# Six modulation chunks of layer 0 moved ahead of the latent attention

## Chip, cores and metric

The kernel runs on one core of a Trainium2 chip. The metric is the device time of one execution in microseconds (us). The time before is 2217.39 us, the median of three runs from 2213.5 to 2222.52 us. The profile shown here is of one further execution, which took 2211.2 us; its trace covers a span of 2209.4 us.

The engines are named as in the profile: PE is TensorE's matmul, PEld its weight load, DVE is VectorE, ACT is ScalarE, POOL is GpSimd and SP is SyncE, which issues most of the DMAs. "Load" below is a DMA from HBM.

## The reference

Two transformer blocks work one after the other on 256 tokens of 1024 features, each with two layers. The change lies in the first layer (layer 0) of the first block, in what feeds its modulation. A conditioning vector `c` (and one for the context tokens, `c_ctx`) is turned into six vectors of 1024 numbers: shift, scale and gate for the mixer, and shift, scale and gate for the feed-forward part.

```python
mod = silu(c) @ w_mod[l] + b_mod[l]          # 1024 -> 6 x 1024
sh1, sc1, g1, sh2, sc2, g2 = split(mod, 6)
u = modulate(rms_norm(h, g_pre_mix), sh1, sc1)
y = even_mixer(u, ...)                        # delta rule + latent attention, then w_out
h = h + g1 * rms_norm(y, g_post_mix)
u = modulate(rms_norm(h, g_pre_ffn), sh2, sc2)
h = h + g2 * rms_norm(swiglu(u, ...), g_post_ffn)
```

The mixer of layer 0 is made of two parts that share one input projection: a gated delta rule in both directions over chunks of 64 tokens, a recurrence with eight heads, and a multi-head latent attention (MLA). Their outputs are concatenated and multiplied by `w_out`.

## The kernel before

Context and latent tokens are handled together as four tiles of 128 tokens. A product of a float32 input and a weight is done as three matmuls on parts cut in two (`mm3`, L554 to L556): a weight tile is loaded by SP, cast to its high part by ACT (L270), and VectorE or GpSimd subtracts to get the low part (L272).

The modulation of layer 0 is done in chunks of 512 columns, numbered 0 to 11; `n // 2` is the vector that a chunk belongs to, in the order shift, scale, gate of the mixer, then of the feed-forward. `mod_chunk` (L361) computes one. It loads `w_mod` in four loads of 512 KB (L370), each into a weight buffer of the tag `wraw`. Each load is used by two float32 matmuls (L373; the trace shows four records for them) whose stationary side is 32 columns wide, with the first two columns the two conditioning vectors; the eight matmuls of a chunk go round the four groups of 32 rows of one PSUM bank, `gv`. ACT copies the bank out (L375). For a gate (chunks 4, 5, 10, 11) a small matmul adds the four groups up (L379), POOL loads the bias (L381), VectorE adds it (L382) and multiplies by a gain (L400), and POOL stores the row to DRAM (L401). For a shift or scale (the others) four small matmuls (L386) give columns, and VectorE adds the bias (L389) and writes the coefficients (L413 or L415).

Chunks 0 to 3 (shift and scale of the mixer) are done at the start, since the first norm needs them. Chunks 4 to 9 (gate of the mixer, shift and scale of the feed-forward) are done in `l0_mixer`, in the loop that the change moves. Chunks 10 and 11 follow later, on VectorE.

In the program, `l0_mixer` goes: input norm, small input projection, delta-rule preparation (`gdn_conv`, `gdn_gate`, `gdn_matrices`), inversion of the triangular matrices (`gdn_invert`), the recurrence of eight steps for each tile and direction (`gdn_run`) and its end (`gdn_post`); then `l0_mla`, then the chunks. `layer0` goes on with `gdn_out` and the output projection (`linear_tok` on `w_out_even`, L1896).

The order on an engine is not that of the program. The kernel is built with

```python
with tile.TileContext(nc, schedule_with_timeline_sim=True) as tc:
```

so a scheduler lays the instructions of each engine in a fixed order when the kernel is built; the order in which the program issues the work enters into it, but does not alone decide it. Each engine then carries out its list in that order. Two resources matter here. From L1850 on, the weight buffers are only the two of the pool `w`, so a load waits until the one before the last has been used. The PSUM pool has one `gv` bank; `mod_chunk` and the attention both use it (in `attend`, L700 puts the reciprocal sums there), and they take it in the order of the program.

In the second half of `gdn_matrices` SP loads two tiles `gE` for each token tile (L1050), VectorE multiplies (L1056) and SP stores the products as `Qd` (L1058). The recurrence loads them again, one 256 KB load `gQ` for each step (L1172).

Of the kernel before, what the change touches and what calls it, by code (L numbers as in the profile page):

```python
# [128 lines left out]
def sbt(K, shape, dt=F32, tag=None, bufs=1, pool=None):  # L129
    return (pool or K.sb).tile(shape, dt, name=nm(K, tag or "u"), tag=tag or nm(K, "one"), bufs=bufs)  # L130
# [69 lines left out]
def bank(K, kind):  # L200
    kind = K.alias.get(kind, kind)
    return K.ps[kind].tile([128, 512], F32, name=nm(K, kind), tag=kind, bufs=K.kinds[kind])
# [158 lines left out]
def mod_chunk(K, W, pool, l, n, pm=None):  # L361

    nc = K.nc
    pm = pm or pool
    ps = bank(K, "gv")
    for g in range(0, 8, KG):
        raw = W.raw()
        nc.sync.dma_start(raw, K.ins["w_mod"][l][g * 128:(g + KG) * 128, n * 512:(n + 1) * 512].rearrange("(k p) n -> p k n", p=128))  # L370
        for k in range(KG):
            j = (g + k) % 4
            nc.tensor.matmul(ps[32 * j:32 * j + 32, :], K.cl[:, g + k, :], raw[:, k, :], start=(g + k < 4), stop=(g + k >= 4))  # L373
    row = sbt(K, [128, 512], F32, "mrow", 1, pm)
    nc.scalar.copy(row, ps)  # L375
    sel = K.c("sel")
    ps = bank(K, "gv")
    if n // 2 in (2, 5):
        nc.tensor.matmul(ps[:2, :], sel, row, start=True, stop=True)  # L379
        b = sbt(K, [128, 512], F32, "mrow", 1, pm)[:2]  # L380
        nc.gpsimd.dma_start(b, K.ins["b_mod"][l, n * 512:(n + 1) * 512].partition_broadcast(2))  # L381
        nc.vector.tensor_tensor(b, ps[:2, :], b, op=ALU.add)  # L382
        mod_gate(K, pool, l, n, b, 2)
        return
    for f in range(4):
        nc.tensor.matmul(ps[:, 2 * f:2 * f + 2], row[:, f * 128:(f + 1) * 128], sel, start=True, stop=True)  # L386
    v = sbt(K, [128, 4, 2], F32, "mcols", 2, pm)
    b = K.col("b_mod")[:, l * 48 + 4 * n:l * 48 + 4 * n + 4]
    nc.vector.tensor_tensor(v, ps[:, :8].rearrange("p (f s) -> p f s", s=2), bc(b, [128, 4, 2], 2), op=ALU.add)  # L389
    mod_cols(K, l, n, v.rearrange("p f s -> p (f s)"), 2)  # L390


def mod_gate(K, pool, l, n, ps, ns):

    nc = K.nc
    i, half = n // 6, n % 2
    cs = slice(half * 512, half * 512 + 512)
    g = sbt(K, [2, 512], F32, "mgr", 1, pool)[:ns]
    nc.gpsimd.dma_start(g, K.ins["g_post"][l, i, cs].partition_broadcast(ns))
    nc.vector.tensor_tensor(g, ps[:ns, :], g, op=ALU.mult)  # L400
    nc.gpsimd.dma_start(K.grow[l][i][:ns, cs], g)  # L401


def mod_cols(K, l, n, ps, ns):

    nc = K.nc
    sec, half = divmod(n, 2)
    f0 = sec * 8 + half * 4
    dst = K.modc[l][:, :ns, f0:f0 + 4]
    src = ps[:, :4 * ns].rearrange("p (f s) -> p s f", s=ns)  # L410
    if sec in (1, 4):
        gain = K.col("pre")[:, (l * 2 + sec // 3) * 8 + half * 4:(l * 2 + sec // 3) * 8 + half * 4 + 4]
        nc.vector.scalar_tensor_tensor(dst, src, 1.0, bc(gain, [128, ns, 4], 1), op0=ALU.add, op1=ALU.mult)  # L413
    else:
        nc.vector.tensor_copy(dst, src)  # L415
# [318 lines left out]
def bc(ap, shape, axis):  # L734
    return ap.unsqueeze(axis).to_broadcast(shape)
# [481 lines left out]
def gdn_run(K):  # L1217
    K.owritten = set()
    for i in range(4):
        for d in range(2):  # L1220
            t = i if d == 0 else (1, 0, 3, 2)[i]
            ops = gdn_operands(K, d, t)
            for a in ((0, 1) if d == 0 else (1, 0)):
                gdn_state(K, d, i == 0 and a == d, t, a, *ops, K.S[d])
# [562 lines left out]
def l0_mixer(K, W, Om):  # L1787
    nc = K.nc
    with Pool(K, "c0") as c0:
# [8 lines left out]
        with Pool(K, "qkv"):  # L1798
            K.small = cut(K, [128, 4, 448])
            K.qkv = [cut(K, [128, 4, 512]) for _ in range(3)]  # L1800
            with Pool(K, "pq") as pP:
# [55 lines left out]
                with Pool(K, "g3"):  # L1857
                    gdn_run(K)
                    gdn_post(K)
                    with Pool(K, "mla", "right"):  # L1860
                        l0_mla(K, Om)
                        for n in range(4, 10):
                            mod_chunk(K, W, K.po, 0, n)


def layer0(K):
# [5 lines left out]
    with Banks(K, {"g": 3, "s": 2, "tp": 1, "po": 1, "gv": 1}, {"acc": "s", "aux": "g"}):  # L1872
        l0_mixer(K, W, Om)
# [297 lines left out]
```

## Time and profile before

| | |
|---|---|
| time of the runs (median of 3) | 2217.39 us |
| the profiled execution | 2211.2 us |
| its span in the trace | 2209.4 us |
| PE busy | 2035.4 us, 92% of the span |
| VectorE busy | 1319.9 us, 60% |
| ScalarE busy | 921.9 us, 42% |
| mean granted clock of PE | 0.936 of full speed |

The page shows the span in 40 slices of 55 us, with one digit each for an engine's busy share in tenths and for the clock granted to PE. A busy PE is not always PE at its peak: matmuls are pipelined, and at a granted clock of 0.5 it counts as busy with half the work done. In timelines, each line gives the start, the duration, the engine, the source line, what is written and read, and how many instructions were put together; in brackets is the engine's idle time before it and what ended it. Source lines are those of the kernel before.

### The profile page before, as it was taken

How to read it: one execution, taken by the hardware profiler on the slowest of the kernel's cores; microseconds unless marked ns; L12 is line 12 of the kernel's file. 1: busy time of each engine (PE TensorE's matmuls, PEld its weight loads, DVE VectorE, ACT ScalarE, POOL GpSimd, SP SyncE). 2: the span in 40 equal slices, each digit the busy share in tenths (PEclk: the TensorE clock that was granted, in tenths of full speed). 3: DMA queues.
4: the chain of work that ended last, by engine and by line, in shares of the span. 5: the costliest groups of instructions: out<-in, count | busy, mean ns of one | idle time of the engine just before them, and what ended most of it. 6: DMA issues, size and time to landing. Idle time of an engine off the chain costs nothing.

```text
span 2209.4 us, 31163 instructions
## 1 busy us (share of the span) xinstructions
PE 2035.4 (92%) x11656; PEld 1640.6 (74%) x11656; DVE 1319.9 (60%) x2737; ACT 921.9 (42%) x1612; POOL 241.2 (11%) x312
## 2 busy tenths in 40 slices
PE   6989898857999999979987999999899999989998
PEld 3777677614887877867656888898688879868886
DVE  5665566702678674463856556585675467566644
ACT  4533433402522223443435544455454345545532
POOL 2211112100100000020311000210200021020000
PEclk9999599957999999989969999999899999989999
DMA  8343300155267663222304557350566535145561
GB/s 273 91 111 82 116 11 16 59 170 171 85 204 234 223 200 105 96 88 67 96 20 152 154 151 241 111 145 20 162 198 188 158 117 162 44 153 167 185 190 68
DMA packets 186952, 291.90 MB, mean 132 GB/s; under 512 B 28472, under 2 KB 75704, under 8 KB 186800
## 3 DMA queue, kind: packets, MB, share of 16 engines
q1 hardware_dynamic: 172720, 272.54, 39.6%
q0 software_dynamic: 5472, 16.13, 2.2%
q10 hardware_dynamic: 8608, 1.23, 0.4%
q8 instruction: 92, 1.51, 0.3%
q14 instruction: 60, 0.49, 0.1%
HBM read 281.44 MB, written 8.41 MB: 131 GB/s over the span
## 4 chain that ended last, share of the span: by engine, by line
PE 81%; DVE 6%; DMA 5%; issue 3%; ACT 3%; POOL 1%; SPq 0%; ACTq 0%; DVEq 0%; POOLq 0%
PE acc L554 18%; PE acc L556 18%; PE acc L555 18%; PE s L554 2%; PE s L555 2%; PE s L556 2%; PE gv L373 2%; DMA wraw<-in_w_mod_dram 2%; PE po L1531 1%; PE tp L1531 1%; PE po L690 1%; PE tp L891 1%; PE aux L729 1%; PE aux L489 1%; PE g L1200 1%
## 5 line engine op out<-in xcount | busy, mean ns | idle before, releaser
L272 DVE TENSOR_TENSOR wlo<-wraw,whi 128x512 fp32r<-128x512 f32 (+4 forms) x772 | 483.1, 669 | 301.2 <-ACT whi L270 284.4
L270 ACT CAST whi<-wraw 128x1024 fp32r<-128x1024 f32 (+4 forms) x420 | 413.6, 990 | 491.2 <-PE acc L556 204.2
L554 PE MATMUL acc<-whi,u 128*128 128x512 f32 (+3 forms) x1320 | 511.5, 390 | 21.5 <-ACT whi L270 13.2
L555 PE MATMUL acc<-wlo,u 128*128 128x512 f32 (+3 forms) x1320 | 509.4, 388 | 0.8 <-DVE wlo L272 0.7
L556 PE MATMUL acc<-whi,u 128*128 128x512 f32 (+3 forms) x1320 | 507.9, 386 | 1.5 <-DVE u L307 1.5
L554 PEld LDWEIGHTS acc<-whi,u 128*128 128x128 f32 x1320 | 253.2, 192 | 72.7 <-ACT whi L270 15.1
L556 PEld LDWEIGHTS acc<-whi,u 128*128 128x128 f32 x1320 | 252.6, 191 | 51.7 <-DVE u L307 3.8
L555 PEld LDWEIGHTS acc<-wlo,u 128*128 128x128 f32 x1320 | 252.7, 192 | 51.2 <-DVE wlo L272 3.6
L554 PE MATMUL acc<-u,whi 128*128 128x512 f32 (+1 forms) x480 | 169.5, 360 | 1.8 <-ACT u L306 1.7
L556 PE MATMUL acc<-u,wlo 128*128 128x512 f32 (+1 forms) x480 | 170.1, 358 | 0.0
L555 PE MATMUL acc<-u,whi 128*128 128x512 f32 (+1 forms) x480 | 169.4, 355 | 0.2 <-DVE u L307 0.2
L272 POOL TENSOR_TENSOR wlo<-wraw,whi 128x512 fp32r<-128x512 f32 (+1 forms) x68 | 83.7, 1261 | 417.4 <-ACT whi L270 417.4
L432 DVE SCALAR_TENSOR_TENSOR msum<-mraw,u,msum 128x512 f32<-128x512 f32 x140 | 100.7, 745 | 12.8 <-DMA mraw<-in_w_mod_dram 11.7
L554 PEld LDWEIGHTS acc<-u,whi 128*128 128x128 f32 x480 | 89.5, 189 | 16.9 <-issue 2.6
L555 PEld LDWEIGHTS acc<-u,whi 128*128 128x128 f32 x480 | 90.4, 188 | 15.2 <-issue 1.7
L556 PEld LDWEIGHTS acc<-u,wlo 128*128 128x128 f32 x480 | 90.1, 188 | 15.1 <-issue 1.7
L307 DVE TENSOR_TENSOR u<-aux,u 128x512 fp32r<-128x512 f32 (+2 forms) x96 | 59.4, 632 | 44.0 <-ACT u L306 44.0
L373 PE MATMUL gv<-wraw,u 128*32 128x512 f32 x160 | 50.2, 900 | 32.2 <-DMA wraw<-in_w_mod_dram 24.6
L306 ACT CAST u<-aux 128x512 fp32r<-128x512 f32 (+2 forms) x96 | 50.4, 543 | 55.7 <-PE aux L729 35.8
L554 PE MATMUL acc<-whi,dxh 128*128 128x512 f32 x176 | 69.7, 396 | 1.9 <-ACT dxh L306 1.9
L555 PE MATMUL acc<-wlo,dxh 128*128 128x512 f32 x176 | 69.6, 396 | 0.0
L556 PE MATMUL acc<-whi,dxl 128*128 128x512 f32 x176 | 69.0, 396 | 0.0
(510 smaller groups left out, 3115.2 us busy)
## 6 DMA issues: line engine op xcount, KB each, us to landing
wraw<-in_w_up_dram SPq DMA_DIRECT2D x64, 512.0 KB, 4.2
wraw<-in_w_down_dram SPq DMA_DIRECT2D x64, 512.0 KB, 4.3
mraw<-in_w_mod_dram SPq DMA_DIRECT2D x56, 512.0 KB, 4.8
wraw<-in_w_ffn_down_dram SPq DMA_DIRECT2D x44, 512.0 KB, 3.8
wraw<-in_w_mod_dram SPq DMA_DIRECT2D x40, 512.0 KB, 4.8
wraw<-in_w_ffn_gate_dram SPq DMA_DIRECT2D x48, 256.0 KB, 3.0
wraw<-in_w_ffn_up_dram SPq DMA_DIRECT2D x48, 256.0 KB, 3.3
wraw<-in_w_ffn_gate_dram SPq DMA_DIRECT2D x20, 512.0 KB, 4.3
```

The source lines that it names most:

```text
L270: self.K.nc.scalar.copy(hi, raw)
L272: e.tensor_tensor(lo[:, k], raw[:, k], hi.bitcast(F32)[:, k], op=ALU.subtract)
L306: (hi_eng or nc.scalar.copy)(hi, src)
L307: nc.vector.tensor_tensor(lo, src, hi.bitcast(F32), op=ALU.subtract)
L373: nc.tensor.matmul(ps[32 * j:32 * j + 32, :], K.cl[:, g + k, :], raw[:, k, :], start=(g + k < 4), stop=(g + k >= 4))
L432: nc.vector.scalar_tensor_tensor(accs[s], raw[:, k, :], c, accs[s], op0=ALU.mult, op1=ALU.add)
L489: nc.tensor.matmul(ps[:, k * 128:(k + 1) * 128], xk, dg, start=True, stop=True)
L554: mm(ps, ah, bh, start=start, stop=False)
L555: mm(ps, ah, bl, start=False, stop=False)
L556: mm(ps, al, bh, start=False, stop=stop)
L690: nc.tensor.matmul(po[hh * 64:hh * 64 + 64, c:c + 128], v(hh, j), pts[hh][0][:, j * 128:(j + 1) * 128], start=(j == 0), stop=(j == nj - 1))
L1531: nc.tensor.matmul(ps[t][:, c * 128:c * 128 + 128], yp[:, c, t * 128 + j:t * 128 + j + 128] if j < 31 else ones, dg, start=(j == 0), stop= ...
```

## The change

The loop over chunks 4 to 9 stands ahead of the call of `l0_mla` instead of behind it.

```diff
                     with Pool(K, "mla", "right"):
-                        l0_mla(K, Om)
                         for n in range(4, 10):
                             mod_chunk(K, W, K.po, 0, n)
+                        l0_mla(K, Om)
```

No instruction is added or taken away. The scheduler puts the chunks' instructions elsewhere on each engine. On SP, in the second half of `gdn_matrices`, this is one piece of the difference between the two lists (`wraw` are weight buffers, `gE` and `Qd` as above; a number is that of a buffer):

```order
 L1050 DMA gE_1837<-Ed_91 128x512
+L370 DMA wraw_3253<-in_w_mod_dram 128x2x512
+L370 DMA wraw_3257<-in_w_mod_dram 128x2x512
 L1058 DMA Qd_79<-gQ_1833 128x512
+L1050 DMA gE_1875<-Ed_90 128x512
 L1058 DMA Qd_83<-gQ_1839 128x512
-L1050 DMA gE_1875<-Ed_90 128x512
 L1050 DMA gE_1881<-Ed_94 128x512
+L370 DMA wraw_3273<-in_w_mod_dram 128x2x512
+L370 DMA wraw_3277<-in_w_mod_dram 128x2x512
 L1058 DMA Qd_82<-gQ_1877 128x512
```

Four of the modulation loads now stand between the loads of gE and the stores of Qd. On PE, at the same place in the program, a modulation matmul (`gv` its bank) stands between the transposes (`tp`) and the products of the delta rule (`g`):

```order
 L1033 MATMUL tp_1843<-const_id_75,u_138 128x128 x4
 L1033 MATMUL tp_1850<-const_id_75,u_137 128x128 x4
+L373 MATMUL gv_3244<-wraw_3253,u_124 32x512 x2
 L1045 MATMUL g_1857<-gT_1855,gT_1848 64x64
 L1045 MATMUL g_1858<-gT_1855,gT_1848 64x64
```

This is the second half of chunk 5; the matmuls of the six chunks are spread in this way from the last gate projections to the fourth step of the recurrence. At the end of the mixer SP now has the loads of the output projection (`w_out_even`) among the last loads of the recurrence (`gQ`), where the modulation loads used to follow:

```order
 L1172 DMA gQ_2771<-Qd_81 128x512
+L276 DMA wraw_4451<-in_w_out_even_dram 128x2x512
+L276 DMA wraw_4458<-in_w_out_even_dram 128x2x512
+L276 DMA wraw_4465<-in_w_out_even_dram 128x2x512
 L1172 DMA gQ_2879<-Qd_86 128x512
 L1172 DMA gQ_2987<-Qd_82 128x512
 L1172 DMA gQ_3095<-Qd_85 128x512
-L370 DMA wraw_4213<-in_w_mod_dram 128x2x512
-L370 DMA wraw_4217<-in_w_mod_dram 128x2x512
```

Three loads of the output projection moved ahead of the last three gQ loads, and no modulation load is left behind these.

## Rows read from the trace of the kernel before

**Rows 1.** The page's 40 slices of the span: PE's busy tenths, and the clock granted to PE in tenths.

```profile
PE   6989898857999999979987999999899999989998
...
PEclk9999599957999999989969999999899999989999
```

**Rows 2.** Busy time by stretch: the stretch and its length in us, busy us and instructions of PE, PEld, DVE, ACT and POOL, then the granted clock, the busy share of the DMA engines and GB/s.

```profile
188.00:217.00 29.00, 26.38 (x154) 22.52 (x153) 10.57 (x16) 5.71 (x9) 4.76 (x4) 1.00 0.52 99
217.00:239.00 22.00, 11.94 (x228) 8.87 (x226) 5.75 (x15) 7.75 (x17) 6.63 (x22) 0.76 0.48 158
239.00:287.00 48.00, 46.07 (x757) 40.38 (x759) 30.69 (x106) 24.59 (x53) 4.53 (x6) 0.61 0.19 62
287.00:312.00 25.00, 23.07 (x220) 18.39 (x215) 17.13 (x29) 9.11 (x23) 3.49 (x5) 0.86 0.08 20
312.00:434.00 122.00, 110.47 (x1041) 88.05 (x1041) 86.87 (x159) 46.42 (x117) 27.20 (x37) 0.94 0.09 25
434.00:514.90 80.90, 48.47 (x149) 13.50 (x149) 9.41 (x19) 8.45 (x15) 4.78 (x9) 0.58 0.52 167
514.90:540.00 25.10, 17.57 (x51) 12.41 (x52) 10.90 (x17) 8.24 (x10) 2.96 (x2) 0.72 0.63 217
540.00:565.00 25.00, 25.00 (x119) 20.77 (x118) 14.46 (x50) 7.97 (x21) 0.00 (x0) 1.00 0.14 43
```

**Rows 3.** PE's timeline from 432 to 516 us.

```profile
432.94 1.09 PE L690 MATMUL po<-pt,u 128*64 128x128 f32 x14
433.96 1.07 PE L373 MATMUL gv<-wraw,u 128*32 128x512 f32 x8
...
439.19 1.05 PE L373 MATMUL gv<-wraw,u 128*32 128x512 f32 x4 [3.15 <-DMA wraw<-in_w_mod_dram]
...
444.55 1.02 PE L379 MATMUL gv<-mrow,const_id 128*2 128x512 f32 x2 [0.69 <-ACT mrow L375]
448.85 1.93 PE L373 MATMUL gv<-wraw,u 128*32 128x512 f32 x8 [3.28 <-DVE mrow L382]
...
473.70 1.87 PE L386 MATMUL gv<-const_id,mrow 128*128 128x2 f32 x8 [0.73 <-ACT mrow L375]
...
482.03 1.92 PE L373 MATMUL gv<-wraw,u 128*32 128x512 f32 x4 [2.27 <-DMA wraw<-in_w_mod_dram]
484.75 1.92 PE L373 MATMUL gv<-wraw,u 128*32 128x512 f32 x4 [0.80 <-DMA wraw<-in_w_mod_dram]
...
513.18 1.86 PE L386 MATMUL gv<-const_id,mrow 128*128 128x2 f32 x8 [0.74 <-ACT mrow L375]
514.91 0.77 PE L554 MATMUL acc<-whi,u 128*128 128x512 f32 x1
```

**Rows 4.** The modulation matmuls of line 373 on PE between 395 and 560 us: the group, and what ended PE's idle time before them (us, times).

```profile
L373 PE MATMUL gv<-wraw,u x96: 592/1061/1062, 434.0 to 511.4; 128*32 128x512 f32 x96
...
  DMA wraw<-in_w_mod_dram: 20.9, 8
  DVE mrow L382: 6.2, 2
```

**Rows 5.** The waits of the SP queue between 434 and 515 us: us in total, times, longest.

```profile
SPq L370 <- PE gv L373: 112.0, 19, 72.0
```

**Rows 6.** PE's timeline in the kernel's first stage, where chunks 0 to 3 stand between transposes (L772); and, last, a weight load behind a modulation matmul at 434.95 us.

```profile
21.07 1.05 PE L373 MATMUL gv<-wraw,u 128*32 128x512 f32 x4
22.06 1.09 PE L772 MATMUL s<-const_id,u 128*128 128x128 f32 x8
...
29.46 1.05 PE L386 MATMUL gv<-const_id,mrow 128*128 128x2 f32 x8 [0.74 <-ACT mrow L375]
...
434.95 0.85 PEld L1253 LDWEIGHTS aux<-const_id,u 128*128 128x128 f32 x8 [0.84 <-issue]
```

**Rows 7.** The chain of work that ended last, from 215 to 245 us: start, duration, what.

```profile
223.35 3.56 DMA gE<-Ed
...
230.02 3.27 DMA gE<-Ed
...
235.54 3.19 DMA gE<-Ed
```

**Rows 8.** DMA issues by line: the first from 208 to 245 us, the second from 434 to 514 us; times, KB each, median us from issue to landing.

```profile
gE<-Ed SPq DMA_DIRECT2D x6, 256.0 KB, 3.3
...
wraw<-in_w_mod_dram SPq DMA_DIRECT2D x22, 512.0 KB, 4.1
```

**Rows 9.** ScalarE at the end of the attention and behind it, from the timeline, and the page's group of the weight casts (count, busy us, mean ns, then idle before).

```profile
433.47 2.18 ACT L306 CAST u<-u 128x512 fp32r<-128x512 f32 x4
...
441.33 0.59 ACT L306 CAST u<-aux 128x512 fp32r<-128x512 f32 x1 [4.61 <-PE aux L1253]
...
L270 ACT CAST whi<-wraw 128x1024 fp32r<-128x1024 f32 (+4 forms) x420 | 413.6, 990 | 491.2 <-PE acc L556 204.2
```

**Rows 10.** The SP queue's timeline from 250 to 560 us: issues of one line are put together, with the time from the first to the last.

```profile
254.97 108.13 SPq L1172 DMA_DIRECT2D gQ<-Qd  x8
435.05 70.88 SPq L370 DMA_DIRECT2D wraw<-in_w_mod_dram  x22
509.55 3.30 SPq L276 DMA_DIRECT2D wraw<-in_w_out_even_dram  x2
```

**Rows 11.** PE's timeline where the attention first uses the bank gv.

```profile
301.47 0.80 PE L700 MATMUL gv<-const_id,rs 128*128 128x128 f32 x2
```

## The prediction

> **What bounds the kernel now.** I read the slices of the page first. TensorE (PE) is busy in most of the 40 slices; the thin ones show as a dip in its busy digits with a low granted clock beside it. The dip in the ninth and tenth slice, some 440 to 550 us, falls in the stage that the change touches [rows 1]. The table by stretch then dates it: from 434.0 to 514.9 us PE is busy 48.47 of 80.9 us, and at a mean granted clock of 0.58, so mostly at 1.2 GHz; before it, 312 to 434 us, it is busy 110.47 of 122 us at 0.94 [rows 2]. PE's timeline says what the stretch is: the last matmul of the latent attention (L690) starts at 432.94 us and lasts 1.09 us, then there is almost nothing but the six modulation chunks (L373, L379, L386), and the first matmul of the output projection (L554) comes at 514.91 us [rows 3]. Within it PE waits 20.9 us for the weight loads and 6.2 us for the bias addition of the two gate chunks [rows 4], and the sync queue (SP) waited 112.0 us in 19 waits for a matmul to give back one of the two buffers (72.0 of them in one wait that began long before the stage) [rows 5]. So the stage is a round trip: load, multiply, free the buffer, load again. Nothing else is left to run beside it, and every one of its 80.9 us is on the path that sets the end.
>
> **What the change takes away.** The order of the changed program has the chunks' matmuls spread over the delta-rule work, from the last gate projections (about 188 us in this trace) to the fourth of its eight steps (about 312 us), and all 24 loads of 512 KB ahead of the fifth of the eight gQ loads. Behind the latent attention stands the output projection at once. Gone are 434.0 to 514.9 us: minus 80.9 us.
>
> **What it adds on PE.** When the four column groups are fed together, two loads cost 1.07 us at the upper clock (433.96 us, 8 records) and 1.93 at the lower (448.85 us); a load that stands alone costs 1.05 or 1.92; the selector matmuls of a chunk cost 1.02 (L379) or 1.87 us (L386, lower clock); for L386 at the upper clock I use 1.05, from the kernel's first stage [rows 3, 6]. By stretch, with the clocks of rows 2:
> 188 to 217 us (clock 1.00): two pairs, 2.1 us.
> 217 to 239 (0.76): one pair, two single loads, two L379, priced at the upper clock: 1.07 + 2.10 + 2.04 = 5.2 us.
> 239 to 287 (0.61, priced at the lower): three pairs, two single loads, two times L386: 5.8 + 3.8 + 3.7 = 13.4 us.
> 287 to 312 (0.86, priced at the upper): three pairs, two single loads, two times L386: 3.2 + 2.1 + 2.1 = 7.4 us.
> Together 28.1 us. PE has room only between 217 and 239 us, where it is busy 11.94 of 22.0 us; from 239 to 312 it is busy 69.1 (46.07 + 23.07) of 73 us [rows 2]. So I hide the 5.2 us of that stretch and put 22.9 us on the path. Bounds: 0, if the 28.1 us of idle that PE has in all of 188 to 434 us (29.0 + 22.0 + 48.0 + 25.0 + 122.0 less the busy time) take it all; 28.1 if nothing hides.
>
> **What the moved loads do in the queue.** Between 220 and 240 us the path is not PE's: the chain steps through three gE loads (3.56, 3.27 and 3.19 us) that SP issues and VectorE waits for [rows 7]. The change puts four of the 512 KB loads among them, on the same queue, each waiting for a matmul to free its buffer. Behind such a wait stand the Qd stores and the next gE load, then VectorE's products, then PE's next g bank. A gE load lands 3.3 us after its issue, a modulation load 4.1 us [rows 8]; two loads issued together were used 2.72 us apart (482.03 and 484.75 us) [rows 3]. So a load in front costs between 0 and 2.72 us; I take 2, since it lies nearer to that row, and 8 us for four. On ScalarE the six L375 copies go between other copies, on GpSimd four short DMA issues and their waits come before the small key work of the attention; ScalarE is busy 7.75 of 22 and 24.59 of 48 us in the two stretches, GpSimd 6.63 and 4.53 [rows 2], so I put 0 on them; if every copy delayed its engine's next work on the path, it would be six times the 0.59 of a 128x512 cast, 3.5 us [rows 9].
>
> Further on, PE itself meets a load that has not landed wherever a pair follows its predecessor closely (about 226 and 296 us in this trace's time). Bounds: 0, and the 20.9 us of rows 4 if the round trip is as bare as before. I take 4 us, near the low end, because elsewhere the next pair stands 7 us or more behind, against 4.1 us to landing.
>
> **The seam and the projection.** After the last attention matmul ScalarE has four casts (2.18 us from 433.47), then two weight casts of 0.99, then the cast of the first transposed features (0.59): 433.47 + 2.18 + 1.98 + 0.59 = 438.2 us, so the projection starts 4.2 us after 434.0 [rows 9]. On the other side, three of its eight loads now start before the attention ends. Before, PE idled 7.5 us of the projection's first 25.1 us (17.57 busy), because its loads only began at 509.55 us [rows 2, 10]. I take 4 us off, about half, bounds 0 and 7.5.
>
> **The sum.** Minus 80.9, plus 22.9, plus 8, plus 4, plus 4.2, minus 4: minus 45.8 us. The profiled execution took 2211.2 us, 1.8 more than its span of 2209.4. So 2165.4 us against 2211.2, a ratio of 0.979; the median of the runs shown is 2217.39, and the same ratio gives 2171. I forecast 2170 us.
>
> **Two rules weighed.** The kernel's modulation matmuls use 32 columns of the array and their neighbours 128, and the trace shows a 32-column group and the transposes behind it without a gap (21.07 us plus 1.05, next start at 22.06), while the weight load behind such a group once came 0.84 us late with no matmul delayed [rows 6]. The Trainium skill, "TensorEngine Tiling (Array Packing)", section Key Properties, states that changing the tiling mode drains the engine; this speaks against scattering the chunks, since there are some 24 such changes instead of a few. By the row the sum stays as it is; by the rule, with 0.84 us as an estimate of a drain, it would be the second rival below.
>
> The granted clock was 0.58 in the stage of before and 0.94 in the attention before it [rows 2]. The Trainium skill, "TensorE: Matmul & The Clock Gate", section What's actually happening, says that the throttled clock is the default and that activity releases it; the trace agrees. Its result would be the first rival below.
>
> **Rivals.**
> *The chunks vanish.* From 239 to 287 us PE was almost always busy, with small matmuls, at 0.61 [rows 2]. If the added 512-column matmuls lift that stretch to the upper clock, its 46.07 us would shrink to about 28 (times 0.61), or the idle time takes all the added work: without the 22.9 us the time is 2171 - 23 = 2148, and with the clock's 18 us in whole 2130. Against it: the same matmuls stood at the lower level, at their 1.92 us, from 448 to 514 us [rows 3].
> *Drains.* If each of the some 24 changes between 32-column and 128-column work holds PE for the 0.84 us by which a weight load was late [rows 6], the time is 2171 + 20 = 2191. For it speaks that row, against it that no matmul waited there and that the first stage has such changes without a gap. The page named above has the rule.
> *The round trip moves along.* If every pair is waited for as before, 20.9 + 6.2 us [rows 4] instead of 4 and nothing hides (5.2), the time is 2171 + 23 + 5 = 2199.
> *Slower.* The sync queue is the place. Eight loads for which the delta rule waits, three gE of the chain and five gQ, now stand behind modulation loads that wait for PE. If PE by then waits for the same step, each of the eight pays its own landing of 3.3 us, a modulation load's 4.1 and 2.72 for the second of the pair [rows 3, 8]: 81 us, 2171 + 81 = 2252. It decides against the change once a step loses 5.8 us (46 / 8). For it: SP carries out its list in order, and before it issued all gQ loads between 254.97 and 363 us with none of the modulation loads among them [rows 10]. Against it: most of these L370 wait for a matmul that stands well ahead of the step.
> *No change.* The order is fixed when the kernel is built and the listing shows it moved, so the change does do what it says; the gain could only be given back afterwards, by attention pairs that start later, as they share the gv bank with the chunks. To give back 35 us or more they would have to be held by that bank until far past the chunks' end at 312 us, while their first use of it now (L700) is at 301.47 us [rows 11].
>
> **How the numbers follow.** Forecast (2150 to 2192): 0.56. The chunks vanish (2130 to 2150): 0.17. Drains (2191): 0.04. The round trip moves along (2192 to 2206): 0.11. No change (2206 to 2228): 0.06. Slower: 0.06. About 0.5%, 11 us, is what a measurement of this kernel can tell from no change. Faster is 0.56 + 0.17 + 0.04 + 0.11 = 0.88. The range from 2138 to 2206 leaves out some 0.07 on the fast side and the 0.12 of the last two cases.
>
> **What will show it.** Right: no stretch in which PE has only L373 between the attention and the projection; L373 in pieces between the delta-rule steps; the attention's last L690 at about 469 us (434 plus 35) instead of 434; the projection about 4 us behind it. The queue term is right if the three gE loads and the products behind them end some 8 us later than the PE work put in before them explains. Wrong: L373 with waits for its loads of over 20 us in all; SP waits of several us ahead of gE or gQ; attention pairs that wait for the gv bank; or a clock above 0.8 in the stretch that ran at 0.61.

## The result and the profile after

The changed kernel takes 2149.72 us, the median of 4 runs (2141.66 to 2151.92), against 2217.94 us for the kernel before beside it (4 runs, 2213.5 to 2222.52): ratio 0.969, interval 0.965 to 0.972. Timed again it gave 2150.69 us, ratio 0.969 (0.965 to 0.972). That is 68 to 70 us less; the forecast was 2170, or 47 less than the median shown.

The two profiled executions of the changed kernel differ: 2141.66 us (span 2139.8) and 2150.13 us (span 2148.4). I call them the first and the second; the second lies at the median.

The page's slices of the first, which answer to [rows 1]:

```profile
PE   6989799899999999799798999998999999989998
...
PEclk9999899899999999899689999998999999989999
```

The thin ninth and tenth slices with their clock digits 5 and 7 are gone (9 and 9 now), and the fifth digit of the clock row, some 215 to 270 us, rose from 5 to 8. The table by stretch, first execution, with the columns and stretches of [rows 2] and one row for all of 188 to 440 us:

```profile
217.00:239.00 22.00, 14.41 (x157) 7.82 (x156) 6.32 (x15) 5.87 (x11) 3.90 (x6) 0.92 0.58 189
239.00:287.00 48.00, 43.35 (x841) 31.03 (x839) 30.15 (x105) 26.52 (x59) 8.09 (x25) 0.82 0.58 184
287.00:312.00 25.00, 23.72 (x222) 17.27 (x223) 16.02 (x30) 9.62 (x22) 4.70 (x7) 1.00 0.41 130
312.00:434.00 122.00, 114.14 (x1100) 91.32 (x1101) 90.52 (x169) 47.73 (x119) 29.96 (x42) 0.94 0.18 59
188.00:440.00 252.00, 228.84 (x2529) 173.59 (x2527) 158.38 (x341) 99.62 (x227) 52.12 (x84) 0.93 0.37 112
```

and the second execution of the same program:

```profile
217.00:239.00 22.00, 14.09 (x155) 7.88 (x153) 5.82 (x14) 5.40 (x10) 4.20 (x6) 0.84 0.53 178
239.00:287.00 48.00, 43.05 (x803) 30.52 (x800) 29.10 (x104) 23.85 (x54) 8.09 (x25) 0.72 0.55 177
188.00:440.00 252.00, 228.03 (x2460) 173.42 (x2458) 152.75 (x333) 93.72 (x214) 52.49 (x84) 0.89 0.37 112
```

The row to look at is 239 to 287 us: the clock there was 0.61 before [rows 2] and is now 0.82 or 0.72, with the modulation matmuls added to it. The kernel before has this row for 188 to 440 us, against which the last row of each is read:

```profile
188.00:440.00 252.00, 220.78 (x2404) 179.32 (x2402) 155.30 (x330) 96.31 (x222) 46.60 (x74) 0.86 0.20 55
```

PE's timeline of the first execution has the chunks in pieces between 190 and 315 us, and the seam behind the attention, to be read against [rows 3]:

```profile
201.21 1.07 PE L373 MATMUL gv<-wraw,u 128*32 128x512 f32 x8
...
234.14 1.92 PE L373 MATMUL gv<-wraw,u 128*32 128x512 f32 x4 [4.46 <-DMA wraw<-in_w_mod_dram]
237.64 1.05 PE L373 MATMUL gv<-wraw,u 128*32 128x512 f32 x4
...
247.03 1.93 PE L373 MATMUL gv<-wraw,u 128*32 128x512 f32 x8 [1.48 <-DVE mrow L382]
...
271.97 1.07 PE L373 MATMUL gv<-wraw,u 128*32 128x512 f32 x8
...
437.14 1.09 PE L690 MATMUL po<-pt,u 128*64 128x128 f32 x14
...
442.28 0.79 PE L554 MATMUL acc<-whi,u 128*128 128x512 f32 x1 [2.47 <-ACT u L306]
```

The attention ends at 438.23 us (437.14 plus 1.09), 4.2 us later than the 434.03 before; in the second execution its last L690 ends at 447.56 us, 13.5 later. The prediction had 469. The group of line 373 between 150 and 400 us, first execution, answers to [rows 4]:

```profile
L373 PE MATMUL gv<-wraw,u x96: 592/617/1062, 190.0 to 315.0; 128*32 128x512 f32 x96
its engine sat idle before it (us, times) until:
  DMA wraw<-in_w_mod_dram: 6.0, 3
  DVE mrow L382: 1.8, 2
```

PE's waits for the loads fell from 20.9 to 6.0 us, and the median matmul from 1061 to 617 ns: most of them now run at the upper clock. From the attention's end to the projection it is 4.1 us in the first and 4.0 in the second execution (442.28 - 438.23, 451.60 - 447.56).

The account, span against span, with all terms from these rows: in the first execution -80.9 (the stage), +4.2 (later end of the attention), +4.1 (the seam), +3.0 (everything behind the first projection matmul: 1697.5 us now, 1694.5 before), together -69.6. In the second -80.9 + 13.5 + 4.0 + 2.3 = -61.1 (spans: 61.0). So the removed stage is gone in full, and the question is why some 27 us of added PE work (20.4 of line 373, 2.0 of L379 and 4.1 of L386 in the first execution), with its loads and waits, move the attention's end by 4 to 13 us and not by the 35 of the forecast.

### The profile page after: what moved, and what is told of

Read it like the earlier page. It is cut to its first block, busy times and chain, and to the rows that moved or that the text cites. A ratio compares the mean times of both kernels' runs of the same rounds, so it can differ in the third digit from the quotient of the medians.

```text
span 2139.8 us, 31171 instructions
## 1 busy us (share of the span) xinstructions
PE 2003.9 (94%) x11656; PEld 1629.7 (76%) x11656; DVE 1318.1 (62%) x2737; ACT 923.5 (43%) x1614; POOL 241.2 (11%) x312
## 4 chain that ended last, share of the span: by engine, by line
PE 85%; DVE 6%; DMA 4%; ACT 3%; issue 2%; ACTq 0%; POOL 0%; SPq 0%; DVEq 0%; POOLq 0%
PE acc L554 19%; PE acc L556 19%; PE acc L555 19%; PE s L554 2%; PE s L555 2%; PE s L556 2%; PE po L690 2%; PE tp L891 2%; PE po L1531 1%; PE tp L1531 1%; DMA wraw<-in_w_mod_dram 1%; PE gv L373 1%; DVE wlo L272 1%; PE tp L679 1%; PE aux L729 1%
## 5 line engine op out<-in xcount | busy, mean ns | idle before, releaser
L554 PE MATMUL acc<-whi,u 128*128 128x512 f32 (+3 forms) x1320 | 510.2, 389 | 17.8 <-ACT u L306 11.2
L554 PEld LDWEIGHTS acc<-whi,u 128*128 128x128 f32 x1320 | 252.1, 191 | 68.0 <-ACT u L306 13.7
L554 PE MATMUL acc<-u,whi 128*128 128x512 f32 (+1 forms) x480 | 170.0, 361 | 1.8 <-ACT u L306 1.7
L554 PEld LDWEIGHTS acc<-u,whi 128*128 128x128 f32 x480 | 90.1, 189 | 17.0 <-issue 2.6
L554 PE MATMUL acc<-whi,dxh 128*128 128x512 f32 x176 | 69.7, 396 | 1.9 <-ACT dxh L306 1.9
L555 PE MATMUL acc<-wlo,dxh 128*128 128x512 f32 x176 | 69.6, 396 | 0.0
L307 DVE TENSOR_TENSOR dxl<-u,dxh 128x1024 fp32r<-128x1024 f32 x22 | 26.7, 1224 | 52.8 <-ACT dxh L306 52.8
```

What stands on the lines that cost most here:

```text
L307: nc.vector.tensor_tensor(lo, src, hi.bitcast(F32), op=ALU.subtract)
L554: mm(ps, ah, bh, start=start, stop=False)
L555: mm(ps, ah, bl, start=False, stop=False)
```

## Theories

**A. The clock pays.** The moved matmuls, 512 columns wide, stand where PE was thin or busy with small matmuls at the lower clock; with them PE is granted the upper clock for more of the stretch, and the delta rule gives back much of what they cost.

**B. Idle time.** They stand where PE waited anyway; the clock has nothing to do with it.

**C. Another order.** The program is put in order when the kernel is built, by a simulation, and the changed place gave another order of everything around; that order gained what the chunks cost.

The size of the order's part matters for the experiments themselves: any edit of the program text reshuffles hundreds of instructions. For five of them the edit is therefore made on the finished list of instructions, after it was ordered, so that each instruction and each wait stays in its place.

## Experiments

**Narrow matmuls, small loads, both, in the order of the changed kernel.** The edit, behind the ordering (`ops` is the ordered list; the condition on the buffer's number picks chunks 4 to 9; the first replacement alone is `a_narrow`, the second `a_small` with the matmuls reading the 64 columns eight times, both are `a_both`; with narrow matmuls the copy L375 repeats their 64 columns, which is left out here):

```diff
+        if line == 373 and int(str(o.memref)[2:].split("_")[0]) > 400:
+            ops[k] = i.__replace__(ins=[ap(a, (1, 64))] + list(i.ins)[1:], outs=[ap(o, (1, 64))])
...
+        if line == 370 and "w_mod" in str(a.memref) and (a.offset % 6144) // 512 in range(4, 10):
+            ops[k] = i.__replace__(ins=[ap(a, (786432, 2), (1, 64))] + list(i.ins)[1:], outs=[ap(o, (512, 2), (1, 64))])
```

> The changed kernel with every instruction in its place, but the matmuls of the six moved chunks read 64 columns of each loaded tile instead of 512 (the copy behind them repeats the 64): about 22 us of PE work gone, loads and waits as they were. Left out: seven eighths of the product of chunks 4 to 9. Theory A (the wide matmuls held the clock up between 242 and 304 us, and the delta rule gave back what they cost): mean granted clock in 242 to 290 us back from 0.82 to 0.70 or less, last attention matmul within 3 us of the 438.2 of the changed kernel, time 2145 to 2153. Theory B (they stood in idle time, the clock has nothing to do with them): clock stays near 0.82, attention ends 433 to 438, time 2144 to 2150. Theory C (the builder's other order of the rest gained some 20 us, and the chunks cost those): clock stays near 0.82, attention ends 414 to 422, time 2125 to 2133.

> The changed kernel with every instruction in its place, but the 24 loads of the moved chunks bring 64 columns (64 KB) instead of 512, and the matmuls read these 64 columns eight times: PE work, waits and order as they were. Left out: seven eighths of the weights of chunks 4 to 9. If the loads cost the 8 us in front of the gE loads and the 4 us of late data that the prediction put on them: attention ends some 12 us before 438.2, time near 2138. If they cost next to nothing: attention ends within 3 us of 438.2, time 2145 to 2151. The granted clock in 242 to 290 us stays at 0.82 or above in either case by theory A.

> Both edits at once on the changed kernel: 64 columns in matmuls and loads, every instruction in its place; the chunks cost neither PE work nor transfers. By theory A the clock falls as in the run with narrow matmuls (0.70 or less in 242 to 290 us), the attention ends at 425 to 436 us, near the 434.0 of the kernel before, and the time is within 10 us of the changed kernel. By theory B the same times at a clock near 0.82. By theory C the attention ends at 405 to 415 us and the time is near 2120.

Measured: `a_narrow` 2142.83 us, ratio 0.965 (0.963 to 0.968); `a_small` 2143.32, 0.965 (0.961 to 0.968); `a_both` 2134.6, 0.961 (0.959 to 0.964). `a_narrow` lies just under the times of theories A and B and 10 us above those of C, `a_small` between its two forecasts, and `a_both` 15 us under the changed kernel, where no more than 10 was expected. Stretches of `a_narrow`:

```profile
239.00:287.00 48.00, 44.45 (x789) 38.69 (x787) 28.64 (x102) 22.25 (x50) 8.09 (x25) 0.50 0.49 163
188.00:440.00 252.00, 228.59 (x2490) 185.31 (x2488) 155.80 (x337) 95.83 (x220) 52.64 (x84) 0.85 0.37 112
```

of `a_small`:

```profile
239.00:287.00 48.00, 43.52 (x845) 30.65 (x841) 30.16 (x105) 26.82 (x59) 8.09 (x25) 0.85 0.32 97
188.00:440.00 252.00, 231.84 (x2533) 174.84 (x2532) 159.92 (x346) 99.63 (x229) 52.56 (x84) 0.93 0.26 72
```

and of `a_both`:

```profile
239.00:287.00 48.00, 44.77 (x823) 39.03 (x820) 31.07 (x108) 26.77 (x59) 8.81 (x26) 0.68 0.27 79
188.00:440.00 252.00, 227.85 (x2534) 184.48 (x2532) 162.49 (x348) 102.51 (x231) 52.89 (x84) 0.88 0.26 72
```

With the same order, loads and waits, taking seven eighths of the columns away puts the clock of 239 to 287 us from 0.82 (0.72) down to 0.50, wholly the lower level. `a_both`, as narrow, has 0.68 there, only 0.04 under the second execution of the changed kernel: with one trace each, the two groups lie apart, but not by much. PE's last L690 in `a_narrow` is this one:

```profile
442.44 1.09 PE L690 MATMUL po<-pt,u 128*64 128x128 f32 x14
```

So with some 14 us less PE work the attention ends at 443.5 us, between the 438.2 and the 447.6 of the two executions with all of it. Theory C wanted 414 to 422 and falls. Theory B wanted the clock to stay and falls as the whole story. Theory A's forecast of the clock (0.70 or less) holds; its 438.2 within 3 us is missed by 2.3, and `a_narrow` is 7 to 8 us quicker by the medians (the intervals overlap), so that the clock gives back all that the wide matmuls cost isn't shown.

Since the clock differs from execution to execution, I set the ends side by side with it taken out. Counting starts at the first key transpose (L1033, from PE's timeline), as some executions are up to 7 us late before that. "Given to the lower clock" is one minus the granted clock of the 188 to 440 row, times 252 us; as the clock has two digits it is good to 1.3 us. It counts PE's idle time at the lower clock as if it were work, so the column is an estimate, and a high one. For `dummy`, whose attention ends earliest, it is taken over its own 206.7 us (a row below), because the clock behind its end, 429.7 to 440 us, is 0.72.

| kernel | L1033 | attention ends | length | granted | given to the lower clock | rest |
|---|---|---|---|---|---|---|
| before | 217.6 | 434.0 | 216.4 | 0.86 | 35.3 | 181.1 |
| after, first | 219.5 | 438.2 | 218.7 | 0.93 | 17.6 | 201.1 |
| after, second | 219.8 | 447.6 | 227.8 | 0.89 | 27.7 | 200.1 |
| `a_small` | 222.0 | 440.0 | 218.0 | 0.93 | 17.6 | 200.4 |
| `a_narrow` | 218.6 | 443.5 | 224.9 | 0.85 | 37.8 | 187.1 |
| `a_both` | 218.6 | 434.9 | 216.3 | 0.88 | 30.2 | 186.1 |
| `dummy` (below) | 223.0 | 429.7 | 206.7 | 0.91 | 18.6 | 188.1 |

The last column falls into groups. Wide matmuls add 14 us to it (200 to 201 against 186 to 187), whatever the loads. Loads add nothing that shows in it: 200.4 with 64 KB, 200.1 and 201.1 with 512 KB. All else that the change brought (selector matmuls, copies, the other order) is 2 to 5 us (186 against 181.1, and against 181.0 and 183.7 in `b_small` and `b_narrow` below, which are the kernel before up to there). The two executions of the changed kernel differ by 9.1 us in length and by 10.1 in what the lower clock took.

That loads add nothing to this column doesn't make them free. With narrow matmuls the small loads take 8 us off the time: every run of `a_both` (at most 2139.26 us) is quicker than every run of `a_narrow` (at least 2141.68). In the traces the lengths differ by as much, 224.9 and 216.3, and the table books it under the clock. With wide matmuls the small loads take 6 to 7 us off the medians, but the intervals overlap. Wide columns and bytes together cost 15 to 16 us at their new place (2149.72 and 2150.69 against 2134.6), and there the intervals don't overlap.

**The wide matmuls twice.** Before's chunks stay where they were, and 48 matmuls without loads are put in at the place of the change:

```diff
                     with Pool(K, "mla", "right"):
+                        stay = sbt(K, [128, KG, 512], F32, "stay", 1, K.po)
+                        nc.gpsimd.memset(stay, 0.001)
+                        for n in range(6):
+                            ps = bank(K, "gv")
+                            for g in range(8):
+                                j = g % 4
+                                nc.tensor.matmul(ps[32 * j:32 * j + 32, :], K.cl[:, g, :], stay[:, g % KG, :], start=(g < 4), stop=(g >= 4))
                         l0_mla(K, Om)
                         for n in range(4, 10):
```

> The kernel before, its six chunks behind the attention as they were, and in the place where the change puts them 48 wide matmuls into the bank gv on a tile that stays resident (no loads, no copies, results unused): the PE work of the chunks is done twice. Theory A: granted clock in 239 to 287 us rises from 0.61 to 0.75 or more, attention ends at 434 to 441 us, time 0 to 8 us over the kernel before. Theory B: clock stays near 0.61, attention ends at 434 to 441 us. Neither (the wide matmuls stand on the path in full, at the lower clock): attention ends at 455 to 470 us, time 20 to 35 us over the kernel before.

Measured: 2217.79 us, ratio 0.999 (0.997 to 1.001): no difference. The group of the added matmuls (they have line 1867 there, and each stands in the trace as two records; PE is busy with them for 11.5 us), and three stretches of this kernel:

```profile
L1867 PE MATMUL gv<-stay,u x96: 592/592/617, 224.3 to 239.0; 128*32 128x512 f32 x96
```

```profile
217.60:242.00 24.40, 23.04 (x248) 11.74 (x247) 5.63 (x14) 6.35 (x11) 8.86 (x24) 1.00 0.33 117
239.00:287.00 48.00, 42.43 (x876) 36.24 (x868) 32.22 (x110) 27.43 (x60) 4.52 (x6) 0.79 0.30 90
223.02:429.68 206.66, 189.73 (x2329) 148.59 (x2331) 140.13 (x307) 87.91 (x209) 42.79 (x71) 0.91 0.16 49
```

All of them stand between 224 and 240 us, where PE had waited for the gE loads: it is busy 23.0 of 24.4 us there at full clock, and in 239 to 287 us the clock is 0.79 and not 0.61 (nor the 0.69 and 0.64 of `b_small` and `b_narrow`). The attention ends at 429.7 us, earlier than the 434 to 441 expected and 4.4 us earlier than without the added work; counted from L1033 it is 9.7 us shorter. Here both A and B are at work: by the table, "rest" rose by 7 us, so part of the 11.5 us stood in idle time, and the lower clock took 16.7 us less. The whole executions bear out the clock: the mean granted clock is 0.937 over the ten of `dummy` and 0.932 over the thirteen of the kernel before that were timed beside it, some 10 us of 2218.

**What held the removed stage.** The same two edits behind the ordering of the kernel before, one execution each.

> The kernel before with every instruction in its place, but the 24 loads of the six chunks behind the attention bring 64 KB instead of 512 KB (the matmuls read the 64 columns eight times). Left out: seven eighths of the weights of chunks 4 to 9. If the stage of 80.9 us is a round trip of load, multiply, free (the reading of the prediction): the loads' part falls from some 4.1 to 2 us each, the stage shrinks to 55 to 68 us. If it is held by the bytes of the loads: 45 us or less. If it is held by PE at the lower clock alone: 75 us or more.

> The kernel before with every instruction in its place, but the matmuls of the six chunks behind the attention read 64 of the 512 columns; loads as they were. Left out: seven eighths of the product of chunks 4 to 9. Round trip: 24 steps lose some 1 us each, the stage shrinks from 80.9 to 55 to 68 us. Held by the bytes: 75 us or more. Held by PE alone: 45 us or less.

Measured: `b_small` 2204.32 us, and its stage, from the last L690 (436.16 + 1.09) to the first L554, 61.8 us; `b_narrow` 2218.84 us and 69.8 us (442.36 to 512.11). The time of `b_narrow` doesn't show its shorter stage: in this one execution L1033 already stood 5.8 us later than in that of before. Two rows bound the stage of `b_small`:

```profile
436.16 1.09 PE L690 MATMUL po<-pt,u 128*64 128x128 f32 x14
...
499.05 0.79 PE L554 MATMUL acc<-whi,u 128*128 128x512 f32 x1 [1.96 <-ACT whi L270]
```

And what PE waited for before line 373 in `b_narrow`, against the 20.9 us of [rows 4]:

```profile
  DMA wraw<-in_w_mod_dram: 34.0, 14
  DVE mrow L382: 7.4, 2
```

Neither the bytes alone nor PE alone held the stage: an eighth of the bytes takes 19 us off, an eighth of the columns 11, and where PE is quicker it waits longer. That is the round trip, though with narrow matmuls the stage stayed 2 us above the 55 to 68 expected for it. These two also show the kernel before in further executions up to the attention: 218.8 and 219.0 us from L1033 to its end, against 216.4.

**Other places.** The changed kernel again, and three variants (the comments name them): the chunks right behind the gate projections (`gate`), ahead of the inversion (`early2`), and the changed kernel with 24 unused wide matmuls put in ahead of the inversion (`fill3`).

```diff
                             gdn_gate(K, W)
+                        for n in range(4, 10):             # gate
+                            mod_chunk(K, W, c0, 0, n)
                         gdn_norm(K, 0)
...
+                with Pool(K, "mc", "right"):               # early2
+                    for n in range(4, 10):
+                        mod_chunk(K, W, K.po, 0, n)
                 with On(K, g2):
                     gdn_invert(K, *LX)
```

> The changed kernel once more, beside the placements below on the same chip: 2140 to 2152 us; attention ends at 438 us within 2, granted clock in 242 to 290 us near 0.82.

> The six chunks stand right behind the gate projections in the program (ahead of the second key preparation), with the third load buffer that is still open there; by the order all 24 pairs then stand ahead of the first delta-rule step. Theory A (wide matmuls hold the clock up where PE is thin or busy with small matmuls): PE busy in 217 to 242 us rises from 17.3 to 20 us or more, at a clock of 0.95 or more, 242 to 290 us at 0.85 or more; the attention ends 3 to 10 us before 438.2, time 2135 to 2145. Rival (the loads now stand ahead of the gE loads that the chain steps through, with PE waiting): attention ends 4 us or more behind 438.2, time 2150 to 2165, with the delta rule's first step starting later than 263 us.

> The six chunks stand ahead of the inversion in the program, with two load buffers: by the order they end at about the fifth step of the delta rule, most of them somewhat earlier than in the changed kernel. Theory A: clock in 242 to 290 us 0.80 to 0.90, attention ends 434 to 440 us, time within 6 us of the changed kernel. Rival (loads in front of gE): attention ends later than 442 us.

> The changed kernel with 24 more wide matmuls into gv on a resident tile, unused, ahead of the inversion in the program: they stand where PE waits for the gE loads (217 to 242 us), and the chunks behind them. Theory A: clock in 217 to 290 us rises (0.93 and 0.82 now) to 0.90 or more over both, the 12.6 us of added PE work cost 0 or less: attention ends 430 to 440 us, time 2138 to 2150. If PE work is what decides: attention ends at 445 to 452 us, time 2152 to 2165.

Measured: `after2` (the second execution above) 2150.69 us, its attention ending 9.6 us behind the 438 expected and its clock 0.72 instead of 0.82; `gate` 2156.62, ratio 0.972 (0.968 to 0.975); `early2` 2149.37, 0.968 (0.965 to 0.972); `fill3` 2158.91, 0.972 (0.969 to 0.976). None is better than the change, and the hopes of theory A for them were missed: from L1033 the attention ends after 239.4 us in `gate`, 234.7 in `early2` and 239.4 in `fill3`, against 218.7 and 227.8. That `early2` takes no longer in all lies in the next layer, whose attention was 8 to 12 us shorter in that execution than in the two of the changed kernel (below).

`gate` was to show the rival of the queue. The first matmul of the first delta-rule step, in the changed kernel and in `gate`:

```profile
263.24 1.49 PE L1159 MATMUL g<-u,u 64*64 64x64 f32 x32
```

```profile
284.03 1.97 PE L1159 MATMUL g<-u,u 64*64 64x64 f32 x30
```

and what held its SP queue between 200 and 290 us (us in total, times, longest):

```profile
SPq L370 <- PE gv L373: 26.1, 9, 9.5
SPq L934 <- POOL cvo L933: 15.4, 4, 6.9
SPq L276 <- DVE wlo L272: 8.4, 1, 8.4
SPq L370 <- DMA wraw<-in_w_mod_dram: 7.3, 4, 3.8
```

The loads of the chunks wait there for PE with the stores and loads of the delta rule behind them, and the first step starts 21 us later (18 counted from L1033: 61.7 against 43.8). But all 24 loads are multiplied ahead of that step there, and 12 in the changed kernel. The chain of work that ended last steps in `gate` through the matmuls of line 373 (21.2% of 205 to 290 us) and through four of the chunks' own loads, and through no gE or gQ load:

```profile
221.56 3.93 DMA wraw<-in_w_mod_dram
...
236.73 5.88 DMA wraw<-in_w_mod_dram
...
266.51 4.17 DMA wraw<-in_w_mod_dram
...
278.66 3.78 DMA wraw<-in_w_mod_dram
```

So what holds the step back is the chunks' own work and round trip, moved onto the path. That their loads hold up those of the delta rule isn't shown by it. All wide matmuls now stand ahead of that step, and still the clock of 242 to 290 us is 0.61, with PE busy 42.7 of 48 us:

```profile
242.00:290.00 48.00, 42.74 (x700) 26.51 (x701) 11.35 (x46) 17.19 (x40) 0.14 (x1) 0.61 0.62 206
```

So wide matmuls are no guarantee of the upper clock. What sets it apart from the changed kernel I haven't found; the fall begins behind 217 to 242 us, where PE in `gate` is busy 16.96 of 25 us.

In `fill3` the clock over 217 to 242 us is 1.00, as hoped, but over 242 to 262 us it is 0.61, and the time is 8 us longer than that of the changed kernel, with intervals that overlap.

**The bias and a third buffer.** Two edits of the changed kernel that aim at its remaining waits: the gate chunks' bias rows fetched ahead of the weights into a tile of their own, and a third load buffer while the chunks are issued.

```diff
+    if n // 2 in (2, 5):                                       # bias
+        b = sbt(K, [2, 512], F32, "mbias", 1, pm)
+        nc.gpsimd.dma_start(b, K.ins["b_mod"][l, n * 512:(n + 1) * 512].partition_broadcast(2))
     ps = bank(K, "gv")
...
+                        W.add(K.po, 1, 0)                      # buf_a
                         for n in range(4, 10):
                             mod_chunk(K, W, K.po, 0, n)
+                        W.drop()
```

> The changed kernel with one edit: the bias rows of the two gate chunks have a tile of their own and are fetched ahead of the chunk's weight loads, not behind its selector matmul (in the changed kernel that fetch takes 5.5 us on the chain, and the next chunk waits for the bank). If the wait counts: the first chunks end 5 us earlier, attention ends 3 to 8 us earlier than 438 to 448 us, time 2138 to 2146. If the granted clock decides: within 6 us of the changed kernel's 2150, with the attention's end following the time at the lower clock between 188 and 440 us (half of that time over some 421 us).

> The changed kernel with a third load buffer while the six chunks are issued. If the waits of PE for loads (6 to 13 us in the changed kernel) cost what they last: attention ends 5 us or more earlier, time 2137 to 2146. If the loads cost nothing, as the run with 64 KB loads says: within 6 us of 2150, and the attention's end less half the time at the lower clock between 188 and 440 us is again near 421 us.

Measured: `bias` 2147.72 us, ratio 0.967 (0.964 to 0.969); `buf_a` 2149.18, 0.968 (0.965 to 0.972). Neither can be told from the change. So a gain from either wait isn't shown; but the "rest" of the table is 207.5 us in `bias` and 206.4 in `buf_a`, where the expectation had the 200 to 201 of the changed kernel (its 421 us less the start at L1033). Some 6 us were lost to the edit or to the new order that came with it; which of them stays open, and they may hide what was saved.

## Why the prediction was right, and where not

The forecast of 2170 us had the direction and the mechanism, and the time lies within the range of 2138 to 2206. It is 20 us too slow, at the border between its likeliest case (2150 to 2192) and the rival that the chunks vanish (2130 to 2150).

**The stage, -80.9: right.** It is gone in full, and the reading of it as a round trip is shown by `b_small` and `b_narrow`.

**PE work on the path, +22.9: the step that failed.** Its size was near: 14 us for the wide columns plus 2 to 5 for all else, some 16 to 19 by the table's last column. What failed was "239 to 287 (0.61, priced at the lower)", that is, the clock taken as given. I set the rival aside because the same matmuls stood at the lower level in the old stage; but there they had long waits between them, and here other work of PE around them; that this makes the difference is argued, no run tests it. In its place the clock of that stretch rose to 0.82 or 0.72, and over 188 to 440 us the lower clock took 17.6 or 27.7 us instead of 35.3. That is 8 to 18 us less than the forecast reckoned with. Without the wide columns, in the same order, it took 37.8 us (`a_narrow`) and 30.2 (`a_both`), so at least part of it comes with the wide matmuls; the split is an estimate. By whole runs, wide columns and bytes cost 15 to 16 us at the new place, where this term and the two on the loads made 35 (7.8 us of selector matmuls among them, which `a_both` keeps). The Trainium skill, "TensorE: Matmul & The Clock Gate", section What's actually happening, has activity release the throttled clock; `dummy` agrees (0.79 with the added matmuls, 0.61 without), and `gate`, at 0.61 with PE busy 42.7 of 48 us, shows that a busy PE alone doesn't tell the level.

The delta rule itself shows no cost: from its first step to its fifth (first L1159 of each) it was 76.8 us (254.02 to 330.81), and 73.4 in `b_small`; it is 70.6 (263.24 to 333.88) in the first and 75.5 (264.20 to 339.67) in the second execution, with 12 of the chunks' 24 loads multiplied in between.

**Loads in front of gE, +8: too much.** In the same order, the first delta-rule step starts 43.8 us behind L1033 in the changed kernel (263.24 - 219.48) and 41.5 with small loads (263.48 - 221.95): 2.2 us. With narrow matmuls it is 2.8 (41.4 in `a_narrow`, 38.6 in `a_both`). What the loads cost in all, this term and the next together, was put at 12 us; the small loads take 8 us off the time with narrow matmuls and 6 to 7, not clear of the noise, with wide ones. By which way they cost it stays open.

**PE waiting for loads, +4: near in size, its cost not told apart.** The trace has 6.0 us of such waits; `a_small` has 2.0 and ends no earlier once the clock is taken out.

**The seam, +4.2: right**, 4.1 and 4.0.

**The ramp, -4: mis-sized, the bound too.** From the first projection matmul to the first matmul of the next layer's attention (L710) it was 539.7 us, and the same in `dummy`, which keeps the old stage; it is 530.6 and 532.3: -9.1 and -7.4, where I took -4 with 7.5 as the most. The bound counted PE's idle time only, but the projection's start also stood at a clock of 0.72 [rows 2], which is 0.87 and 0.86 in its first 25.1 us now, here in the first and in the second execution:

```profile
442.30:467.40 25.10, 24.01 (x98) 19.26 (x99) 14.63 (x29) 8.83 (x13) 2.55 (x2) 0.87 0.60 189
```

```profile
451.60:476.70 25.10, 23.52 (x94) 18.95 (x95) 13.68 (x27) 8.97 (x13) 2.54 (x2) 0.86 0.62 189
```

That gain isn't seen in the total, because the later stages took 12.1 and 9.7 us longer in these two executions than in the one of before. The change doesn't touch them, so that this hides the gain is chance; most of it lies in the next layer's attention, which from its first L710 to the first L729 behind it lasted 185.9 us in that execution of before, 192.6 in `dummy`, 184.3 in `early2` and 196.1 and 192.6 in the two of after.

**The rivals.** "Drains": everything but the wide columns costs 2 to 5 us in all by the table, so the 20 us that the rule of the Trainium skill, "TensorEngine Tiling (Array Packing)", section Key Properties, would make with 0.84 us a change don't show here. "The round trip moves along": 6.0 + 1.8 us of waits instead of 27.1. "No change": the attention's first use of the bank (L700) comes at 321.3 us instead of 301.5, but PE sat idle before none of its 32 records. "Slower" didn't come: the first step lost 2.2 us to the loads, and the next four together none that shows. With the chunks earlier in the program (`gate`) the first step comes 18 us later, and even then the removed stage outweighs it. Of the signs that I named beforehand as wrong for the forecast, two came. One is the clock above 0.8 in the stretch that ran at 0.61. The other is SP held for several us ahead of gQ loads, between 246 and 340 us in the first execution:

```profile
SPq L370 <- PE gv L373: 25.7, 10, 8.7
```

It was no sign of harm: the start of the fifth step is 3.1 us later than before, that of the first 9.2 (8.9 and 10.2 in the second execution), so nothing was lost between them.

## What to carry to other kernels

Work moved out of a stage that is a bare round trip is gained in full there; what it costs at its new place is not its duration at the clock that stands in the old profile. Where a stretch runs at the lower clock, price added wide matmuls both with the clock as it is and with the stretch lifted, and give the second more than a small chance; `gate` and `fill3` show that it needn't come. To tell an effect from the reshuffling that any edit causes, edit the ordered list of instructions and keep every instruction in its place.

## Unexpected in the hardware

Adding PE work shortened a stage: 48 unused wide matmuls between 224 and 240 us, with the clock of 239 to 287 us at 0.79, against 0.61 to 0.69 in three executions without them, and the end of the attention 9.7 to 12.3 us earlier counted from the same start. And the granted clock is a property of the execution as well: the same program had 0.82 and 0.72 in two executions in the same stretch, and from L1033 to the attention's end it was 9.1 us longer in one, which is as much as most of the edits tried here are worth.
